# One of two transposed copies in a block inverse goes from TensorE to VectorE, and a list scheduler hands urgency on to whoever opens a tile

## The chip, the cores and the metric

The kernel runs on one core of a Trainium2 chip. The metric is device time in microseconds (us) per execution; a time shown for a kernel is the median of several runs. A core has five engines with queues of their own, each of which issues in order: TensorE (PE in the profile, its weight loads PEld), VectorE (DVE), ScalarE (ACT), GpSimd (POOL) and SyncE (SP, which issues the DMA transfers).

## The reference, cut to what matters

One decoder layer for 2048 prompt tokens and 8 single-token samples, width 1024: a mixer (a Conformer convolution beside a gated DeltaNet with 4 heads of 128), cross-attention into 256 memory tokens, a SwiGLU of inner width 2816, and a final norm. The change lies in the chunked DeltaNet, in chunks of 64 tokens:

```python
decay = jnp.exp(jnp.where(incl, gc[..., :, None] - gc[..., None, :], -jnp.inf))
lower = jnp.where(strict, jnp.einsum('nbhid,nbhjd->nbhij', kb, k) * decay, 0.0)
a_mat = lower + jnp.eye(c, dtype=lower.dtype)
u = lax.linalg.triangular_solve(a_mat, v * beta[..., None], left_side=True, lower=True, unit_diagonal=True)
w = lax.linalg.triangular_solve(a_mat, kb * jnp.exp(gc)[..., None], left_side=True, lower=True, unit_diagonal=True)

def step(s, xs):                      # over the chunks, state s
    v_new = u_i - jnp.einsum('bhcd,bhde->bhce', w_i, s)
    o_i = (jnp.einsum('bhcd,bhde->bhce', q_i * jnp.exp(g_i)[..., None], s)
           + jnp.einsum('bhij,bhje->bhie', qk_i, v_new))
    s = s * jnp.exp(g_last)[..., None, None] + jnp.einsum('bhcd,bhce->bhde', k_dec, v_new)
    return s, o_i
```

## The kernel before, in words

**Stages.** The prompt is cut into four blocks of 512 tokens. The matrix work runs on TensorE in this order: the input projection of blocks 0 and 1 and then of 2 and 3 (tiles `hd`, `glua`, `glub`); keys and values of the memory (`mkv`, `wk`, `vp`, with the transposes `pkt`); output projection and attention of blocks 0 and 1 (`rg`, `sc`, `ppt`); SwiGLU of block 0 (`fx`, `fy`, `fz`, then `dn`, `dx`, `dz`); attention of block 2; and so on to the SwiGLU of block 3. Weights come from DRAM into tiles `raw`, which ScalarE and VectorE or GpSimd split into two rounded parts `w`; each product is three matmuls.

**The DeltaNet in between.** For each of 4 heads and 4 blocks a generator `dn_front` (L1819) prepares four pieces of 128 tokens (NT = 4), and `dn_chain` (L2020) then carries the state through them one after the other. So there are 16 fronts and 64 steps of the chain. Their instructions are threaded between the matmuls of the stages above. A step of the chain is a row of links across engines: `pch<-S,kT` on TensorE, `chr` on VectorE, `pch<-chr,W` on TensorE, `chv` on ScalarE, `pch<-chv,..` on TensorE, the new state `S` on VectorE.

**The inverse.** A front solves the triangular system by inverting `a_mat` in tiles `Tm` (the inverse) and `W` (its transpose), both 128x512: first blocks of 16 on VectorE and GpSimd (`base_inverse`), then 32, 64 and 128 wide by two small matmuls per level (`pu1` and `pu2`, both `pu` in the profile). Before the levels from 32 and from 64 the transpose has to be made anew from `Tm`. A helper `renew` (L1939) does it: four 128x128 transposes on TensorE against the identity into a PSUM tile `ptw`, and one ScalarE copy of the 128x512 tile into `W`. It is called at L1969 and L1996. After the first call, `Tm` consists of blocks of 32 by 32 on the diagonal and zeros elsewhere. ScalarE copies behind each call put the pieces side by side.

**What sets the order.** Nothing is issued while the generators run: every instruction is recorded by the class `Tape`. `Tape.order` (L316) is a list scheduler with a planner's clock per engine; it picks, among the instructions that its clock has ready on an engine, the one with the smallest key, and `issue` (L524) then issues all of them in that order, so L530 is the line of nearly all instructions. The key of a TensorE instruction is its place in the recorded program. The key of any other is the smallest of its own place plus LATER = 300, the keys of its successors, and the keys of the instructions that wait for a buffer that it helps to free (`nxt`, in `keys`, L299). An instruction whose tile has no buffer yet opens one: pools are named by a tag and have a number of buffers (`t2` 28, `act` 22, `w` 6, `raw` 11 and small ones), and `may` (L351) lets a tile be opened ahead of earlier ones of its pool only if enough buffers stay for those. An addition, subtraction or product of two SBUF tiles may be given to GpSimd in place of VectorE if VectorE's backlog is over 1800 on the planner's clock.

Of the kernel before, what the change touches and what calls it, by code (L numbers as in the profile page):

```python
# [154 lines left out]
class Tape:  # L155
# [19 lines left out]
        return TapePort(self, real, eng)  # L175

    def add(self, eng, op, fn, args, kw):
        if op in ("matmul", "transpose", "memset"):
            outs, ins = [args[0]], [a for a in args[1:] if hasattr(a, "name")]
        else:  # L180
            outs = [kw[k] for k in ("out", "accum_out") if kw.get(k) is not None]
            ins = [v for k, v in kw.items() if k not in ("out", "accum_out") and hasattr(v, "name") and hasattr(v, "shape")]
        self.ops.append((eng, op, fn, args, kw, outs, ins, self.cost(eng, op, args, kw, outs, ins)))
        two = {"dve": "pool", "pool": "dve"}.get(eng)
        if two in self.real and op == "tensor_tensor" and kw.get("op") in (ALU.add, ALU.subtract, ALU.mult):
            if elems(outs[0]) >= FLEX and not any(a.name in self.psum for a in outs + ins):
                self.other[len(self.ops) - 1] = two, getattr(self.real[two], op), self.cost(two, op, args, kw, outs, ins)
# [108 lines left out]
            tiles.append(list(dict.fromkeys(a.name for a in outs + ins if a.name in self.tag_of)))  # L296
        return preds, tiles

    def keys(self, succs, line, first, tiles):  # L299


        N = len(self.ops)
        nxt = {}
        for tag, ts in line.items():
            for k, t in enumerate(ts[: -self.bufs[tag]]):
                nxt[t] = first[ts[k + self.bufs[tag]]]
        key = list(range(N))
        for n in range(N - 1, -1, -1):
            if self.ops[n][0] != "pe":
                after = [key[m] for m in succs[n]] + [key[nxt[t]] for t in tiles[n] if t in nxt and nxt[t] > n]  # L310
                key[n] = min([n + LATER, *after])
        for n in self.follow:
            key[n] -= N
        return key

    def order(self):  # L316
        from heapq import heapify, heappop, heappush

        preds, tiles = self.graph()
        N = len(self.ops)  # L320
        succs, left = [[] for _ in range(N)], [len(p) for p in preds]
# [13 lines left out]
        for tag, ts in line.items():  # L335
# [3 lines left out]
            for t in ts:  # L339
# [1 line left out]
                    heappop(held)  # L341
                heappush(held, last[t])
                live[tag].append(len(held))
        key = self.keys(succs, line, first, tiles)
        free = {tag: [0.0] * self.bufs[tag] for tag in line}
        head = dict.fromkeys(line, 0)
        early = {tag: set() for tag in line}
# [305 lines left out]
def hybrid_step(ctx: ExitStack, tc: tile.TileContext, i: dict, o: list):  # L653
# [1165 lines left out]
    def dn_front(h, b, sc, prev, out):  # L1819
# [146 lines left out]
            copy(lp[up, :, dn], lt[up, 0:NT:2, dn])  # L1966
            copy(lp[dn, :, up], lt[up, 1:NT:2, dn])
        yield Tm
        yield from renew()  # L1969
        for r in (0, 64):  # L1970
            up, dn = slice(r, r + 32), slice(r + 32, r + 64)
            copy(Tm[dn, 0:NT:2, up], Tm[up, 1:NT:2, up])
# [1224 lines left out]
```

## Time and profile before

| what | value |
|---|---|
| time, median of 3 runs | 2899.41 us (2897.57 to 2899.71) |
| the profiled execution: its time | 2901.18 us |
| the profiled execution: its span | 2899.4 us |
| PE busy | 2854.1 us, 98% of the span |
| DVE busy | 2438.3 us, 84% |
| ACT busy | 1534.5 us, 53% |
| POOL busy | 803.6 us, 28% |
| mean DMA rate | 196 GB/s |
| mean granted clock of TensorE | 0.996 |

The span runs from the first to the last instruction; the execution's own time has 1.8 us around it, and stands 1.8 us above the median of the runs. A busy share is the share of time in which at least one instruction of the engine is under way. Matmuls overlap one another, so a line of the groups with x4 and 0.60 us means four matmuls from the start of the first to the end of the last.

### The profile page before, as it was taken

What the parts mean: (1) busy time and instruction counts of PE and PEld (TensorE: products, weight loads), DVE (VectorE), ACT (ScalarE), POOL (GpSimd) and SP (SyncE); (2) the same over time, 40 slices, a digit from 0 to 9 for tenths busy, and PEclk for the clock granted to TensorE, in tenths of its full rate; (3) what the DMA queues carried; (4) which work ended last, traced back from release to release, by engine and by line L of the source; (5) the groups of instructions that cost most, each with busy time, mean ns of one, the idle gap of its engine ahead of it and who ended that gap; (6) DMA issues with size and microseconds to landing.
All of it is one profiled execution on the core that took longest, in us unless ns stands there. A gap on an engine that the chain in (4) does not pass through costs nothing. (4 is left out here: it accounts for less than half of the span.)

```text
span 2899.4 us, 55713 instructions
## 1 busy us (share of the span) xinstructions
PE 2854.1 (98%) x19302; PEld 2577.1 (89%) x19302; DVE 2438.3 (84%) x5311; ACT 1534.5 (53%) x3444; POOL 803.6 (28%) x965
## 2 busy tenths in 40 slices
PE   9999999999999999999999999999999999999998
PEld 8999878888788888898988789999889999999998
DVE  8859889898758959998888878888867888888888
ACT  7654564557675456475655454444554444444444
POOL 3311253216302026655213810000632242400000
PEclk9999999999999999999999999999999999999999
DMA  6433335777764426756777777777627666676673
GB/s 224 143 107 108 116 122 178 233 251 250 226 225 124 124 90 200 236 168 224 245 245 252 247 240 238 246 234 240 195 84 234 208 211 189 211 235 196 218 212 127
DMA packets 363035, 569.39 MB, mean 196 GB/s; under 512 B 55841, under 2 KB 158561, under 8 KB 362737
## 3 DMA queue, kind: packets, MB, share of 16 engines
q1 hardware_dynamic: 362752, 565.84, 61.0%
q8 instruction: 152, 2.49, 0.4%
q14 instruction: 131, 1.07, 0.1%
HBM read 457.77 MB, written 108.51 MB: 195 GB/s over the span
## 5 line engine op out<-in xcount | busy, mean ns | idle before, releaser
L530 ACT ACTIVATE w<-raw 128x512 fp32r<-128x512 f32 (+1 forms) x1066 | 649.0, 619 | 793.3 <-issue 133.7
L530 DVE TENSOR_TENSOR w<-raw,w 128x512 fp32r<-128x512 f32 (+1 forms) x842 | 593.2, 709 | 181.5 <-ACT w L530 172.2
L530 PE MATMUL fy<-op,w 128*128 128x256 f32 (+1 forms) x3168 | 435.6, 282 | 2.0 <-DMA w<-sums 2.0
L530 PEld LDWEIGHTS fy<-op,w 128*128 128x128 f32 x3168 | 399.9, 188 | 6.9 <-PE fz L530 2.0
L530 POOL TENSOR_TENSOR w<-raw,w 128x512 fp32r<-128x512 f32 (+1 forms) x224 | 311.8, 1397 | 317.5 <-ACT w L530 245.8
L530 PE MATMUL hd<-hT,w 128*128 128x512 f32 (+2 forms) x1920 | 386.3, 354 | 0.6 <-DVE hT L530 0.6
L530 DVE SCALAR_TENSOR_TENSOR cacc<-cu,cw,cacc 128x512 f32<-128x512 f32 x480 | 358.0, 746 | 5.5 <-ACT cacc L530 2.2
L530 PEld LDWEIGHTS hd<-hT,w 128*128 128x128 f32 x1920 | 304.5, 188 | 47.3 <-DVE hT L530 1.2
L530 PE MATMUL fx<-op,w 128*128 128x256 f32 (+1 forms) x2112 | 296.7, 283 | 1.0 <-ACT ffu L530 0.9
L530 PE MATMUL fz<-op,w 128*128 128x256 f32 (+1 forms) x2112 | 287.4, 283 | 1.3 <-DMA w<-sums 1.2
L530 PEld LDWEIGHTS fx<-op,w 128*128 128x128 f32 x2112 | 269.2, 189 | 6.5 <-issue 1.7
L530 PEld LDWEIGHTS fz<-op,w 128*128 128x128 f32 x2112 | 264.7, 188 | 6.2 <-DMA w<-sums 2.3
L530 PE MATMUL dx<-fo,w 128*128 128x256 f32 (+1 forms) x1344 | 198.3, 283 | 2.2 <-DVE x L530 2.2
L530 PE MATMUL dn<-ff,w 128*128 128x512 f32 (+2 forms) x960 | 193.4, 354 | 1.0 <-DVE x L530 0.9
L530 PE MATMUL rg<-pT,w 128*128 128x512 f32 x768 | 191.1, 400 | 1.1 <-ACT pr L530 0.8
L530 PE MATMUL sc<-w,hT 128*128 128x512 f32 x768 | 188.3, 399 | 3.1 <-ACT pr L530 2.7
L530 PE MATMUL rg<-catS,w 128*128 128x512 f32 (+2 forms) x960 | 187.6, 352 | 0.4 <-DVE x L530 0.4
L530 PEld LDWEIGHTS dx<-fo,w 128*128 128x128 f32 x1344 | 174.7, 188 | 5.0 <-DVE x L530 3.6
L530 PEld LDWEIGHTS rg<-catS,w 128*128 128x128 f32 x960 | 154.2, 188 | 24.7 <-DVE x L530 0.6
L530 PEld LDWEIGHTS sc<-w,hT 128*128 128x128 f32 x768 | 141.3, 188 | 36.5 <-ACT pr L530 5.1
L530 PEld LDWEIGHTS dn<-ff,w 128*128 128x128 f32 x960 | 151.6, 189 | 23.0 <-DVE x L530 2.1
L530 PEld LDWEIGHTS rg<-pT,w 128*128 128x128 f32 x768 | 140.6, 188 | 33.3 <-ACT pr L530 2.2
(433 smaller groups left out, 4901.4 us busy)
## 6 DMA issues: line engine op xcount, KB each, us to landing
w<-sums SPq DMA_DIRECT2D x222, 512.0 KB, 4.4
raw<-in_w_gate_dram SPq DMA_DIRECT2D x192, 256.0 KB, 3.7
sums<-w SPq DMA_DIRECT2D x66, 512.0 KB, 3.7
raw<-in_w_up_dram SPq DMA_DIRECT2D x118, 256.0 KB, 3.7
raw<-in_w_down_dram SPq DMA_DIRECT2D x224, 128.0 KB, 2.8
raw<-in_w_in_dram SPq DMA_DIRECT2D x96, 256.0 KB, 3.0
raw<-sums SPq DMA_DIRECT2D x74, 256.0 KB, 3.4
raw<-wk SPq DMA_DIRECT2D x64, 256.0 KB, 3.0
```

What stands on the lines that cost most here:

```text
L530: fn(*args, **kw)
```

## The change

Two edits go in together.

First, the call of `renew` at L1969 is replaced by one VectorE instruction that transposes each block of 32 by 32 of `Tm` where it lies, straight into `W`. The second call, at L1996, stays. So that the tape records a VectorE `transpose` by its keywords, `add` now asks whether positional arguments were given.

Second, `keys` gets the list `live` (how many tiles of the pool are open, in program order, when a tile is opened). For tile number k of a pool with `bufs` buffers it looks up the tile m = k + 1 + bufs - live[k], which is the first later tile that finds no room while tile k has not been opened, and puts the key of the instruction that opens tile m among those from which the opener of tile k takes the smallest. Openers on TensorE keep their place as key.

```diff
     def add(self, eng, op, fn, args, kw):
-        if op in ("matmul", "transpose", "memset"):
+        if args:
             outs, ins = [args[0]], [a for a in args[1:] if hasattr(a, "name")]
...
-    def keys(self, succs, line, first, tiles):
+    def keys(self, succs, line, first, tiles, live):
...
-        nxt = {}
+        nxt, bars = {}, {}
         for tag, ts in line.items():
             for k, t in enumerate(ts[: -self.bufs[tag]]):
                 nxt[t] = first[ts[k + self.bufs[tag]]]
+            for k, t in enumerate(ts):
+                m = k + 1 + self.bufs[tag] - live[tag][k]
+                if m < len(ts) and first[ts[m]] > first[t]:
+                    bars.setdefault(first[t], []).append(first[ts[m]])
         key = list(range(N))
         for n in range(N - 1, -1, -1):
             if self.ops[n][0] != "pe":
                 after = [key[m] for m in succs[n]] + [key[nxt[t]] for t in tiles[n] if t in nxt and nxt[t] > n]
+                after += [key[m] for m in bars.get(n, ())]
                 key[n] = min([n + LATER, *after])
...
-        key = self.keys(succs, line, first, tiles)
+        key = self.keys(succs, line, first, tiles, live)
...
         yield Tm
-        yield from renew()
+        V.transpose(out=W.rearrange("p c i -> p (c i)"), in_=Tm.rearrange("p c i -> p (c i)"))
         for r in (0, 64):
             up, dn = slice(r, r + 32), slice(r + 32, r + 64)
             copy(Tm[dn, 0:NT:2, up], Tm[up, 1:NT:2, up])
```

**What moves.** TensorE loses 64 of its 128 transposes `ptw`, ScalarE 16 of 32 copies `W<-ptw`, and VectorE gains 16 block transposes of 128x512. No other matmul and no transfer is added or dropped. The order differs on every engine in the first part of the program; it is the same again, instruction by instruction, over the last 9220 of 18386 matmuls, the last 2382 of 5313 VectorE instructions, the last 1042 of 3127 on ScalarE, the last 170 of 970 on GpSimd and the last 731 of 2062 transfers (counts of the order before).

**Place A, the first inverse that lies in the SwiGLU of block 0 (the twelfth of 16 before, the thirteenth now).** ScalarE before, with the copy that the change removes (`Tm` and `W` are the inverse and its transpose, `ffu`, `ffs` and `w` belong to the SwiGLU):

```order
L530 ACTIVATE lt_2672<-lt_2672 64x2x64
L530 ACTIVATE w_2853<-raw_2793 128x512
L530 ACTIVATE Tm_2771<-Tm_2771 32x2x32 x2
L530 ACTIVATE W_2816<-ptw_2852 128x512
L530 ACTIVATE W_2816<-W_2816 32x2x32 x2
L530 ACT_TABLE_LOAD
```

VectorE of the change, with the block transpose in its place:

```order
L535 TENSOR_TENSOR ffu_2961<-fz_2963,ffu_2961 128x256
L535 TENSOR_TENSOR Tm_2838<-pu_2766_2964,Tm_2838 128x16x16
L535 TENSOR_TENSOR w_2965<-raw_2920,w_2965 128x512
L535 STREAM_TRANSPOSE W_2936<-Tm_2838 128x512
L535 TENSOR_TENSOR ffs_2962<-ffu_2961,fy_2970 128x256
L535 TENSOR_REDUCE w_2741_2939<-Tm_2938 32x2x2 x2
```

The transpose now follows two instructions behind the sum that completes `Tm`, with one weight split between them, and stands ahead of the SwiGLU's eviction `ffs<-ffu,fy`.

**Place B, a step of the chain behind that inverse, in the same SwiGLU.** TensorE before, at the third of the chain's four steps (`pch` and `po` are the chain, `pkk`, `pqk`, `pu` and `ptw` the fronts, `fy` and `dn` the SwiGLU):

```order
L530 MATMUL pch_2960<-S_2956,kT_2668 128x128
L530 MATMUL pkk_2965<-kT_2916 128x128 x4
L530 MATMUL pch_2960<-chr_2961,W_2816 128x128
L530 MATMUL fy_2933<-op_2529,w_2928 128x256
L530 MATMUL fy_2933<-op_2541,w_2928 128x256 x3
L530 MATMUL fy_2933<-op_2555,w_2928 128x256 x2
L530 MATMUL po_2897<-chv_2967,dn_2667 128x128
L530 MATMUL pu_2770_2968<-u_217,W_2935 128x64 x4
L530 MATMUL pch_2960<-chv_2967,dn_2666 128x128
L530 MATMUL pqk_2971<-qTd_2917,kT_2916 128x128 x4
L530 MATMUL ptw_2973<-ident,Tm_2834 128x128 x4
L530 MATMUL pch_2974<-S_2969,kT_2668 128x128
```

TensorE of the change, at the first step of the chain behind the inverse of place A:

```order
L535 MATMUL pch_3024<-S_1437,kT_2696 128x128
L535 MATMUL dn_3020<-ff_2990,w_2999 128x512 x3
L535 MATMUL dn_3027<-ff_2942,w_2999 128x512 x3
L535 MATMUL dn_3027<-ff_2990,w_2999 128x512 x3
L535 MATMUL pu_2830_3028<-Tm_2938,lo_3026 64x64 x4
L535 MATMUL dn_3030<-ff_2942,w_3000 128x512 x3
L535 MATMUL pch_3024<-chr_3025,W_2936 128x128
L535 MATMUL dn_3030<-ff_2990,w_3000 128x512 x3
L535 MATMUL dn_3032<-ff_2942,w_3000 128x512 x3
L535 MATMUL dn_3032<-ff_2990,w_3000 128x512 x3
L535 MATMUL pu_2835_3033<-u_217,W_2976 128x64 x4
L535 MATMUL fx_3035<-op_2593,w_3002 128x256 x3
```

Between the first two links of the step there stood four short matmuls; now there stand twelve long ones and four short ones.

**Place C, the values of the memory (`vp`).** TensorE before, at a step of the chain beside the ninth inverse:

```order
L530 MATMUL pch_1929<-S_1914,kT_1520 128x128
L530 MATMUL po_1887<-S_1914,rb_1525 128x128
L530 MATMUL ptw_1931<-ident,Tm_1740 128x128
L530 MATMUL vp_1879<-w_1871,kvT_1752 128x512 x3
L530 MATMUL vp_1879<-w_1873,kvT_1752 128x512 x3
L530 MATMUL vp_1881<-w_1871,kvT_1752 128x512 x3
L530 MATMUL vp_1881<-w_1873,kvT_1752 128x512 x3
L530 MATMUL vp_1896<-w_1892,kvT_1752 128x512 x3
L530 MATMUL vp_1896<-w_1895,kvT_1752 128x512 x3
L530 MATMUL ptw_1931<-ident,Tm_1740 128x128 x3
L530 MATMUL pch_1929<-chr_1930,W_1736 128x128
L530 MATMUL lnp_1960<-ident,lnx_1928 128x128 x4
```

TensorE of the change, again at a step beside the ninth inverse:

```order
L535 MATMUL po_1886<-chv_1904,at_1485 128x128
L535 MATMUL pch_1940<-S_1916,kT_1477 128x128
L535 MATMUL pu_1734_1932<-u_217,W_1765 128x64 x2
L535 MATMUL po_1886<-S_1916,rb_1482 128x128
L535 MATMUL pch_1940<-chr_1941,W_1655 128x128
L535 MATMUL ptw_1944<-ident,Tm_1673 128x128 x4
L535 MATMUL po_1886<-chv_1948,at_1485 128x128
L535 MATMUL pch_1940<-chv_1948,kd_1483 128x128
L535 MATMUL pu_1757_1955<-Tm_1673,lt_1585 128x64 x2
L535 MATMUL po_1886<-S_1953,rb_1482 128x128
L535 MATMUL vp_1901<-w_1879,kvT_1736 128x512 x3
```

Here 18 long matmuls stood between two links; now a whole step of the chain passes with no long matmul in it.

**Counted over the whole order.** Each of the 64 steps has two round trips from TensorE back to TensorE (from `pch<-S` over `chr` to `pch<-chr`, and from there over `chv` to `pch<-chv`), 128 in all. With 0.23 us for a matmul of 512 columns, 0.12 for one of 256 and 0.11 for the short ones (the distances between their starts in the trace), 14 round trips have less than 1.1 us of TensorE work between their links before, and 7 with the change. Of the 14, six lie in the SwiGLU of block 0; of the 7, none does. In the stretch of `mkv`, `wk` and `vp` there are 3 before and 4 with the change.

## The prediction, as it was recorded before the result

> **What bounds the kernel now.** I read the engines' shares first, then the busy time by stretches, then the waits of TensorE, and last the lines of the inverse in order of time.
>
> ```profile
> PE 2854.1 (98%) x19302; PEld 2577.1 (89%) x19302; DVE 2438.3 (84%) x5311; ACT 1534.5 (53%) x3444; POOL 803.6 (28%) x965
> ```
>
> TensorE sits idle for 2899.4 - 2854.1 = 45.3 us in all. Nothing that shortens another engine can give more than that; only work taken from TensorE itself, or a lost clock given back, goes beyond it. The stretches say where the idle time lies (columns: PE, PEld, DVE, ACT, POOL busy with counts, granted clock, DMA share, GB/s):
>
> ```profile
> 0.00:1500.00 1500.00, 1473.37 (x9047) 1280.08 (x9048) 1276.89 (x2635) 893.55 (x2130) 501.92 (x722) 0.99 0.57 182
> 1500.00:1600.00 100.00, 99.88 (x599) 85.30 (x599) 85.45 (x138) 53.23 (x119) 32.59 (x28) 1.00 0.76 256
> 1600.00:2800.00 1200.00, 1191.13 (x8910) 1122.68 (x8909) 988.92 (x2317) 544.09 (x1104) 265.26 (x211) 1.00 0.67 213
> 2800.00:2900.00 100.00, 89.69 (x752) 89.04 (x750) 87.07 (x225) 43.59 (x93) 3.86 (x5) 0.97 0.49 153
> ```
>
> Of the idle time, 26.6 us lie before 1500 us, where the DeltaNet runs, 8.9 between 1600 and 2800, and some 10 in the last 100. The order of the change equals the old one over the last 9220 matmuls; 8910 + 752 are issued after 1600 us, so from about 1700 us on nothing is moved. TensorE is busy for 1191.1 of 1200 us there: what is won or lost earlier should come through to the end whole, as a shift.
>
> Within the first part the idle time is uneven, and the granted clock falls short of one in four stretches:
>
> ```profile
> 300.00:400.00 100.00, 96.79 (x565) 79.17 (x565) 85.69 (x179) 59.67 (x148) 44.27 (x66) 0.98 0.40 122
> 600.00:700.00 100.00, 99.63 (x522) 82.70 (x521) 91.45 (x177) 64.12 (x140) 29.03 (x35) 0.98 0.80 255
> 700.00:800.00 100.00, 92.48 (x557) 79.73 (x556) 75.73 (x156) 67.50 (x164) 52.23 (x70) 0.97 0.78 246
> 800.00:900.00 100.00, 97.67 (x687) 89.28 (x687) 71.49 (x155) 66.97 (x159) 15.44 (x23) 1.00 0.60 196
> 1100.00:1200.00 100.00, 97.65 (x616) 87.11 (x614) 97.70 (x165) 55.96 (x131) 70.60 (x65) 1.00 0.72 235
> 1200.00:1300.00 100.00, 97.71 (x731) 91.30 (x730) 95.85 (x200) 63.72 (x167) 55.02 (x76) 1.00 0.63 195
> 1300.00:1400.00 100.00, 97.21 (x670) 88.28 (x669) 90.26 (x180) 56.69 (x145) 54.06 (x57) 0.98 0.63 214
> ```
>
> The worst stretch, 700 to 800 us, is the memory's keys and values (`wk`, `vp`): 7.5 us idle and 3% of the clock. In the SwiGLU of block 0, 1100 to 1300, VectorE is nearly full.
>
> **The transposes that leave TensorE.** The first `ptw` of the trace, in order of time:
>
> ```profile
> 147.45 0.60 PE L530 MATMUL ptw<-ident,Tm 128*128 128x128 f32 x4
> 147.88 0.60 PE L530 MATMUL pq<-ident,qTd 128*128 128x128 f32 x4
> ```
>
> One transpose lasts 0.27 us, but the next group starts 147.88 - 147.45 = 0.43 us after the first, so four of them hold TensorE for 0.43. Sixteen such groups go: 16 x 0.43 = 6.9 us. TensorE is 98% busy in the first 1500 us, so this comes off the path almost whole: **-6.9**. ScalarE loses 16 copies:
>
> ```profile
> L530 ACT ACTIVATE W<-ptw 128x512 f32<-128x512 f32 x32 | 19.2, 599 | 0.7
> ```
>
> That is 16 x 0.60 = 9.6 us on an engine that is 53% busy. It is worth nothing by itself; what it does for the round trips is in the term after next.
>
> **The block transposes that come to VectorE.** No such instruction is in the trace. The nearest rows, 128x256 below and 128x512 above (last but one number: mean ns):
>
> ```profile
> L530 DVE TENSOR_TENSOR raw<-hd,rsb 128x256 f32<-128x256 f32 x24 | 9.4, 414 | 3.7 <-PE hd L530 3.7
> L530 DVE TENSOR_REDUCE scs<-kt 128x2 f32<-128x512 f32 x32 | 20.9, 673 | 4.8 <-POOL kt L530 4.8
> L530 DVE SCALAR_TENSOR_TENSOR xn<-xn,vcol,rsb 128x512 f32<-128x512 f32 x2 | 2.7, 1371 | 0.0
> ```
>
> I take 0.67, the row with one SBUF source and 512 elements; the ends are 0.41 and 1.37. So 16 x 0.67 = 10.8 us (6.6 to 21.9) against 1500 - 1276.9 = 223 us of idle VectorE: covered, but not where VectorE is 96 to 98% busy. Four of the inverses lie in that SwiGLU in the new order. There the transpose stands ahead of `ffs<-ffu,fy` (place A), which frees a PSUM tile that TensorE's next `fx`, `fy` or `fz` needs. If each delays TensorE by its whole length, that is 4 x 0.67 = 2.7 us (5.5 by the upper row); if none does, 0. The transpose's own wait, for the sum that completes `Tm`, is two places ahead on the same engine with a weight split between them, so nothing queues behind an open wait. Even with VectorE full, TensorE was idle for only 2.3 us per 100 there, which speaks for the lower end: **+1.0**.
>
> By the Trainium skill, "VectorE: DVE Perf Modes", section "The three transpose paths", a 128x128 block transpose of 16-bit numbers takes 311 ns on VectorE; four for a 128x512 tile would be an estimate of 1.24 us. No run here shows one. By that the term would be 4 x 1.24 = 5.0 at most and 1.9 in the same proportion, and the sum 0.9 less favourable.
>
> **The round trips.** What TensorE waited for in the DeltaNet (us in total, times, longest):
>
> ```profile
> PE pu L530 <- DMA Tm<-zt: 2.2, 2, 1.5
> PE po L530 <- ACT chv L530: 1.6, 2, 1.1
> PE pch L530 <- DVE chr L530: 1.6, 3, 1.2
> PE pch L530 <- DVE S L530: 1.3, 1, 1.3
> PE ptw L530 <- ACT Tm L530: 1.3, 4, 0.5
> PE pu L530 <- DVE u L530: 0.8, 2, 0.4
> ```
>
> Together 8.8 us. How long a round trip needs, seen where one just fails to fit:
>
> ```profile
> 796.85 0.38 PE L530 MATMUL pch<-S,kT 128*128 128x128 f32 x2
> ...
> 798.03 0.49 PE L530 MATMUL pch<-chr,W 128*128 128x128 f32 x2 [0.19 <-DVE chr L530]
> 798.96 0.43 PE L530 MATMUL pu<-u,W 128*128 128x64 f32 x2 [0.43 <-DVE u L530]
> 799.51 0.49 PE L530 MATMUL po<-chv,at 128*128 128x128 f32 x2
> ```
>
> From start to start 1.18 us over VectorE, so about 1.1 us of other matmuls must stand between two links. In the old order 14 of 128 trips have less, and the missing pieces add up to 6.9 us (3.1 over `chr`, 3.8 over `chv`); in the new order 7 have less, with 3.3 us missing (2.7 and 0.6). The trips of place B are gone; place C has a new one, with 0.3 and 0.5 us where there were 4.7 and 0.5. The ends: 0, if something else fills the gap, and -8.8, if all of these waits go. I take the difference, 3.3 - 6.9: **-3.6**. What would be late next is the weight split that TensorE's next product needs, since the chain no longer holds it back.
>
> **The clock.** Two places where it was lost:
>
> ```profile
> 747.00:753.00 6.00, 3.25 (x24) 2.81 (x25) 5.96 (x16) 2.34 (x6) 3.49 (x5) 0.99 0.34 100
> 753.00:757.00 4.00, 4.00 (x23) 4.00 (x22) 4.00 (x9) 1.47 (x4) 2.60 (x2) 0.58 0.61 215
> 1310.00:1316.00 6.00, 4.47 (x21) 3.37 (x21) 6.00 (x11) 2.54 (x6) 6.00 (x5) 1.00 0.24 71
> 1316.00:1320.00 4.00, 4.00 (x15) 3.41 (x16) 4.00 (x7) 0.00 (x0) 0.77 (x3) 0.57 0.90 294
> ```
>
> After 6 us in which TensorE was busy for only 3.3 or 4.5, the next 4 us are granted 0.57 to 0.58: 1.7 us lost each time. The four stretches above lose 2 + 2 + 3 + 2 = 9 us in all. Which of them come back under the new order the order doesn't tell; I take **0**, with ends of -9 and +5 (three more).
>
> By the Trainium skill, "TensorE: Matmul & The Clock Gate", section "Why this matters for your kernels", the clock falls only for idle gaps over some 3 us. The trace disagrees here, since it fell after pieces of at most 1.3 us:
>
> ```profile
> 748.08 0.49 PE L530 MATMUL pch<-S,kT 128*128 128x128 f32 x2 [1.34 <-DVE S L530]
> 751.20 0.66 PE L530 MATMUL pkt<-ident,kv 128*128 128x128 f32 x4 [1.23 <-ACT kv L530]
> ```
>
> By that rule no rearrangement could win or lose clock, and the rivals below would lose their clock terms.
>
> **The sum.** -6.9 + 1.0 - 3.6 + 0 = -9.5 us. The profiled execution took 2901.18 us, 1.8 around its span of 2899.4; it would take 2891.7. The median of the runs is 1.8 below the profiled one: 2889.9, or 0.33% less. A difference under 0.2%, 5.8 us, can't be told from none here.
>
> **The rivals.**
>
> *More is won.* All 8.8 us of those waits go, and with them three of the clock losses: -6.9 - 8.8 - 3 x 1.7 = -20.8, 2878.6 us. For it: the SwiGLU loses all its tight trips, and four inverses lie there where there were five, under a VectorE that was full. Against it: seven tight trips stay, four of them in the worst stretch.
>
> *Nothing is won.* The loosened trips don't count, because the link behind them is late on VectorE anyway (0); the transposes cost their full 2.7 in the full SwiGLU; one clock loss comes on top (1.7): -6.9 + 2.7 + 1.7 = -2.5, 2896.9. That is also the case in which the new keys do nothing useful. For it: every reordered queue meets its waits anew, and the planner's clock knows nothing of the granted clock. Against it: 6.9 us leave the bounding engine for certain.
>
> *Slower.* The crowding at `wk` and `vp` decides. In the new order the ninth inverse and a whole step of the chain stand there with no long matmul among them (place C), and two tight trips lie in `wk`. From 700 to 900 us, 7.5 + 2.3 us were idle and 3 us of clock lost; if that stretch loses the same again, it is 12.9 us more: -6.9 + 1.0 + 12.9 = +7.0, 2906.4. It decides as soon as the stretch loses over 5.9 us more, about half of what it loses now. For it: the clock falls exactly behind such small idle pieces. Against it: the stretch holds as many steps of the chain as before, six, and one tight trip more.
>
> **How the numbers follow.** The forecast (-4 to -16) has 0.50, of which 0.04 lies within 0.2%; more won 0.14; nothing won 0.22; slower 0.14. So faster 0.46 + 0.14 = 0.60, same 0.04 + 0.22 = 0.26, slower 0.14. The range runs from 2877, which leaves out the better half of the larger gain (0.06), to 2903, which leaves out most of the slower case (0.10). The forecast's own range is 2883 to 2896.
>
> **What would show it.** `ptw` shows 64 matmuls in place of 128 and `W<-ptw` 16 copies; TensorE's busy time falls by some 7 us less what is idle now and filled then; a block transpose takes 0.4 to 1.4 us, most likely 0.67. Idle time before `pch`, `po`, `ptw` and `pu` falls from 8.8 to some 5 us, and none of it lies in the SwiGLU. From 1700 us on the two traces differ by a constant shift. It is wrong if the stretch of `wk` and `vp` shows over 13 us idle or a clock under 0.97, if the block transpose lasts over 1.4 us, or if the second half stretches by more than 3 us.

## The result, and the profile after

The change took **2921.6 us** (median of 6 runs, 2917.0 to 2924.6) against 2899.6 for the kernel before beside it (6 runs): a ratio of **1.0069, 95% interval 1.0059 to 1.0079**, some 20 us slower. The forecast was 2889.9, faster. The profiled span grew from 2899.4 to 2919.2 us, by 19.8.

The engines' shares, of the changed kernel:

```profile
PE 2854.9 (98%) x19238; PEld 2575.5 (88%) x19238; DVE 2482.6 (85%) x5316; ACT 1525.7 (52%) x3427; POOL 822.0 (28%) x976
```

64 matmuls are gone, and yet TensorE is busy for 0.8 us longer (2854.1 before): what was saved is used up by a lower clock. It is idle for 2919.2 - 2854.9 = 64.3 us, where it was 45.3. The stretches say where (PE, PEld, DVE, ACT, POOL busy with counts, granted clock, DMA share, GB/s). Before:

```profile
0.00:600.00 600.00, 593.64 (x3551) 509.06 (x3552) 511.21 (x1116) 348.03 (x792) 172.70 (x321) 1.00 0.49 155
600.00:950.00 350.00, 339.44 (x2011) 291.22 (x2010) 279.92 (x583) 229.03 (x540) 101.59 (x137) 0.99 0.68 217
950.00:1350.00 400.00, 390.91 (x2397) 342.48 (x2396) 352.49 (x671) 222.17 (x575) 178.49 (x207) 1.00 0.53 169
1350.00:1700.00 350.00, 346.30 (x2127) 299.89 (x2126) 306.12 (x541) 193.97 (x444) 147.96 (x130) 1.00 0.71 239
1700.00:2800.00 1100.00, 1094.07 (x8475) 1045.40 (x8474) 901.51 (x2180) 497.66 (x1002) 199.04 (x165) 1.00 0.67 213
```

And with the change:

```profile
0.00:600.00 600.00, 595.37 (x3590) 510.54 (x3591) 515.70 (x1121) 355.28 (x819) 180.94 (x323) 1.00 0.49 156
600.00:950.00 350.00, 328.31 (x1942) 282.72 (x1941) 289.14 (x578) 215.77 (x536) 163.12 (x202) 0.98 0.68 213
950.00:1350.00 400.00, 382.69 (x2242) 330.97 (x2241) 358.03 (x643) 204.34 (x500) 132.17 (x147) 0.99 0.51 163
1350.00:1700.00 350.00, 344.80 (x2163) 301.13 (x2163) 308.83 (x547) 200.86 (x466) 140.32 (x132) 1.00 0.71 237
1700.00:2800.00 1100.00, 1095.21 (x8408) 1042.99 (x8407) 907.32 (x2164) 497.40 (x997) 201.58 (x168) 1.00 0.67 213
```

From 600 to 950 us (the end of the second input projection; the memory's `mkv`, `wk` and `vp`, up to 823 us; then output projection and attention) TensorE is busy for 11 us less. From 950 to 1350 (output projection and attention, and from 1144 us before or 1169 now the first half of the SwiGLU of block 0) it is 8 less. Below, the first of the two is called the memory's stretch. Behind 1700 us little changed. A second thing moved: GpSimd has 202 instructions in the memory's stretch, where it had 137, and 147 in the next, where it had 207. Work of the DeltaNet's fronts has come forward. The matmuls `pkk<-kT`, of which each front issues 8, count the fronts. Before:

```profile
600.00:950.00 350.00, 3.22 (x24) 2.91 (x24) 3.34 (x12) 0.99 0.68 217
950.00:1350.00 400.00, 4.39 (x32) 3.98 (x32) 4.54 (x16) 1.00 0.53 169
```

With the change:

```profile
600.00:950.00 350.00, 5.38 (x40) 4.93 (x40) 5.70 (x20) 0.98 0.68 213
950.00:1350.00 400.00, 2.11 (x16) 1.94 (x16) 2.33 (x8) 0.99 0.51 163
```

Five fronts are prepared in the memory's stretch in place of three, two in the next in place of four. What TensorE waits for now (us in total, times, longest):

```profile
PE pu L535 <- DMA Tm<-zt: 6.3, 3, 4.7
PE fz L535 <- DMA w<-sums: 4.1, 5, 1.5
PE fx L535 <- ACT ffu L535: 3.5, 3, 1.9
PE pqk L535 <- DVE vnk L535: 3.4, 1, 3.4
PE mkv L535 <- ACT kv L535: 3.3, 1, 3.3
...
PE pk L535 <- DVE lt L535: 2.6, 1, 2.6
...
PE dnb L535 <- DVE tbd L535: 2.2, 1, 2.2
...
PE pch L535 <- DVE S L535: 1.0, 1, 1.0
PE pch L535 <- DVE chr L535: 0.7, 2, 0.4
...
PE ptw L535 <- ACT Tm L535: 0.5, 1, 0.5
```

The chain's waits did shrink: `pch`, `po` and `ptw` from 5.8 us to 2.2. In their place stand a few long single waits in the fronts and around them. (Of the 4.1 us of `fz`, 3.1 lie behind 1700 us.) How one comes about, in order of time, on VectorE:

```profile
713.12 0.74 DVE L535 SCALAR_TENSOR_TENSOR cacc<-cu,cw,cacc 128x512 f32<-128x512 f32 x1
713.77 4.84 DVE L535 CAST catS<-hcat 128x8 fp32r<-128x8 f32 x1
718.39 0.82 DVE L535 SCALAR_TENSOR_TENSOR cacc<-cu,cw,cacc 128x512 f32<-128x512 f32 x1
...
720.79 0.68 DVE L535 TENSOR_TENSOR vnk<-pvv,s 128x512 f32<-128x512 f32 x1
```

on GpSimd:

```profile
713.39 1.29 POOL L535 TENSOR_TENSOR w<-raw,w 128x512 fp32r<-128x512 f32 x1
714.63 0.12 POOL L535 MEMSET w<- 32x16 f32 x1
714.70 1.26 POOL L535 TENSOR_TENSOR w<-raw,w 128x512 fp32r<-128x512 f32 x1
715.93 1.27 POOL L535 TENSOR_TENSOR catS<-cat,catS 128x512 fp32r<-128x512 f32 x1
717.17 1.27 POOL L535 TENSOR_TENSOR w<-raw,w 128x512 fp32r<-128x512 f32 x1
```

and on TensorE:

```profile
717.59 0.55 PE L535 MATMUL pu<-u,W 128*128 128x64 f32 x4
721.52 0.83 PE L535 MATMUL pqk<-qTd,kT 128*128 128x128 f32 x3 [3.38 <-DVE vnk L535]
```

A cast of 8 columns lasts 4.84 us on VectorE, up to 718.61. GpSimd's run of four subtractions of 128x512 ends at 717.17 + 1.27 = 718.44, and the cast 0.17 us behind it, which is as long as such a cast takes alone (first series below). The front's `vnk` stands four instructions behind it, and TensorE stands still for 3.4 us. The clock follows:

```profile
717.00:722.00 5.00, 1.62 (x11) 1.35 (x10) 5.00 (x8) 1.49 (x5) 3.05 (x5) 0.97 0.63 216
722.00:726.00 4.00, 4.00 (x20) 3.83 (x20) 3.64 (x11) 1.32 (x4) 0.00 (x0) 0.60 0.60 151
```

Below, an instruction of VectorE is called **held** if it lasts over 2.4 us before 1700 us; the changed kernel has 6 (23.8 us together), the one before 1 (3.7 us). The **loss** of a stretch is TensorE's idle time in it and half of the time for which the clock records show half speed, which comes in steps of 3.4 us. Up to 1700 us the loss went from 38.2 to 64.2 us, 26.0 more; 5.8 us of TensorE's work (busy time less half of the half-speed time) go off, and 0.4 us less is lost behind 1700. That makes the 19.8 by which the span grew. By stages, in us, with the fronts that start in each:

| stage, and where it ends (before / now) | loss before | loss now | fronts before / now |
|---|---|---|---|
| up to 600 | 8.1 | 4.6 | 7 / 7 |
| input projection, to 689 / 684 | 2.1 | 2.0 | 0 / 1 |
| `mkv`, to 748 / 749 | 1.3 | 10.1 | 2 / 1 |
| `wk` and `vp`, to 823 | 11.2 | 7.8 | 0 / 0 |
| output projection and attention, to 950 | 1.1 | 10.4 | 1 / 3 |
| the same, to 1144 / 1169 | 1.7 | 7.4 | 1 / 0 |
| SwiGLU of block 0, to 1350 | 9.1 | 15.0 | 3 / 2 |
| up to 1700 | 3.7 | 6.9 | 2 / 2 |

The loss grows on both sides of `wk` and `vp`, and not in them.

### The profile page after: what moved, and what is told of

It is laid out like the page before. It is cut to its first block, busy times and chain, and to the rows that moved or that the text cites. A ratio compares the mean times of both kernels' runs of the same rounds, so it can differ in the third digit from the quotient of the medians.

```text
span 2919.2 us, 55627 instructions
## 1 busy us (share of the span) xinstructions
PE 2854.9 (98%) x19238; PEld 2575.5 (88%) x19238; DVE 2482.6 (85%) x5316; ACT 1525.7 (52%) x3427; POOL 822.0 (28%) x976
## 5 line engine op out<-in xcount | busy, mean ns | idle before, releaser
L535 DVE TENSOR_TENSOR w<-raw,w 128x512 fp32r<-128x512 f32 (+1 forms) x847 | 606.9, 720 | 152.5 <-ACT w L535 147.7
L535 PEld LDWEIGHTS fz<-op,w 128*128 128x128 f32 x2112 | 265.0, 188 | 10.8 <-DMA w<-sums 5.6
```

Of the source, the lines that this page charges most:

```text
L535: fn(*args, **kw)
```

## The experiments

In the expectations theory P has VectorE held behind GpSimd's runs, theory K has the new keys cost time whatever they act on, and theory S has any rearrangement move the time by chance. Each kernel is compared with the kernel before on its own chip; times in brackets are 95% intervals of the ratio.

**Each part alone, and the lateness bound.** The transposes alone leave the new rule out:

```diff
-                after += [key[m] for m in bars.get(n, ())]
```

> The block transpose alone, with the old keys. Measured so far: 2899.6 us before, 2921.6 with both edits; TensorE idle 45.3 us before, 64.3 after; five half-clock stretches of 3.4 us before 1700 us, then nine. Theory K (the handed-on urgency orders the work badly): 2893 us, the 6.9 us of transposes less some 1 us. Theory T (the transposes on VectorE hold up its queue): 2915 us or more. Theory P (a VectorE instruction is held for 3 to 5 us while GpSimd runs instructions back to back; TensorE waits behind it and its clock halves; how often the two meet is set anew by any other order): the time follows the number of VectorE instructions held over 3 us before 1700 us, of which the kernel before has 1 and the change 6.

The keys alone put the old call back:

```diff
-        V.transpose(out=W.rearrange("p c i -> p (c i)"), in_=Tm.rearrange("p c i -> p (c i)"))
+        yield from renew()
```

> The handed-on urgency alone, with the transposes left on TensorE. Theory K: 2928 us, 6.9 more than with both edits. Theory T: 2899 us or less. Theory P: between 2895 and 2930, and again by the number of held instructions.

Two kernels have neither part, only `LATER = 310` or `290`:

> The kernel before, with LATER = 310 in place of 300: the same work, another order, neither edit. Theory N (any other order loses, since the one before is an unusually good one): 2910 us or more. Theories K and T: 2899 +- 6 us. Theory P: the time follows the number of held VectorE instructions, whichever way it goes.

> The kernel before, with LATER = 290: a second order without either edit. Theory N: 2910 us or more, as with 310. Theories K and T: 2899 +- 6 us. Theory P: by the number of held VectorE instructions.

Then the changed kernel, and the transposes alone, at the other bounds:

> Both edits with LATER = 290. The kernel before took 2916.9, 2901.9 and 2894.9 us with LATER = 290, 300 and 310. Theory K (the handed-on urgency costs time by itself): above the old keys for each value of LATER, here 2925 us or more. Theory R (every order is a draw, with some 10 us of spread, and the new keys are one more): anywhere from 2895 to 2925, not tied to the 2916.9.

> Both edits with LATER = 310. Theory K: 2908 us or more, over the 2894.9 of the old keys with 310. Theory R: anywhere from 2895 to 2925; at or below 2895 would speak against K outright.

> The block transpose alone with LATER = 310, against the 2894.9 us of LATER = 310 without it. If the 6.9 us of TensorE come through: 2888 us. Theory R: 2885 to 2915, since the edit also re-orders everything around it, as with LATER = 300, where it gave nothing (2901.4 against 2901.9).

> Old keys, VectorE's transpose, lateness bound 290: the third pair beside the new keys with the transpose at 290 (2914.6 us). Theory K (the new keys cost 10 to 20 us whatever the order they act on: plus 20 at 300, plus 11 at 310): 2895 to 2905. Theory S (an order's time is spread by chance over some 25 us and the bound of 290 is simply a bad one for the old keys, 2916.9 without the transpose): 2908 to 2918, no more than 7 us from both.

And the keys alone at 310:

> The new keys with TensorE's transposes kept and the lateness bound at 310; the old keys at 310 took 2894.9 us. A second pair without the transposes. Theory K (the new keys cost 10 to 20 us whatever they act on): 2904 to 2916, with 3 held VectorE instructions or more and TensorE's idle time before 1700 us at 34 us or above. Theory S (chance of the order): as near to 2895 as to 2915, 2890 to 2903 being as likely as not.

Measured, ratio to the kernel before and median in us:

| LATER | neither | transposes alone | keys alone | both |
|---|---|---|---|---|
| 290 | 1.0055 (1.0040 to 1.0070), 2916.9 | 1.0013 (1.0004 to 1.0023), 2903.5 | not run | 1.0044 (1.0028 to 1.0060), 2914.6 |
| 300 | 1 | 1.0005 (0.9992 to 1.0017), 2901.4 | 1.0058 (1.0043 to 1.0073), 2918.0 | 1.0069, 2921.6 |
| 310 | 0.9975 (0.9966 to 0.9985), 2894.9 | 1.0006 (0.9997 to 1.0016), 2902.1 | 1.0022 (1.0013 to 1.0032), 2907.2 | 1.0038 (1.0023 to 1.0053), 2912.9 |

A bound moved by 10 in 300, with nothing else changed, moves the time by -7 or +16 us: two rearrangements that aim at nothing move it that far. The new keys cost in all five pairs, by the ratios 9, 19 and 9 us with the transposes and 17 and 14 without. So theory K stands as a direction for these five pairs, with a size that the order sets; the neutral orders scatter as widely, so that the keys must cost time in any order is not shown. Most sizes that were expected missed: theory K's 2893 and 2928 for the parts alone, its 2925 or more for both at 290, its three held instructions for the keys alone at 310 (there was one), and the 2888 for the transposes at 310. Theory T failed both ways, and theory N, which fits 290, failed at 310. The transposes with the order made anew are worth -12, +1 and +9 us on the old keys, +3 and +5 on the new ones: no gain on average, where 6.9 us leave TensorE by the prediction's sum. Losses by stretch in the profiled executions (us), with the fronts in the memory's stretch:

| kernel | fronts, 600 to 950 | GpSimd instructions there | loss 600 to 950 | loss 950 to 1350 | held |
|---|---|---|---|---|---|
| neither, 290 / 300 / 310 | 3 / 3 / 3 | 145 / 137 / 136 | 13.6 / 15.7 / 12.6 | 22.5 / 10.8 / 9.2 | 2 / 1 / 1 |
| keys alone, 300 / 310 | 3 / 3 | 142 / 141 | 14.4 / 17.2 | 26.4 / 16.3 | 3 / 1 |
| transposes alone, 290 / 300 / 310 | 5 / 5 / 5 | 190 / 191 / 188 | 20.4 / 27.2 / 20.0 | 13.5 / 15.8 / 16.3 | 2 / 2 / 1 |
| both, 290 / 300 / 310 | 5 / 5 / 5 | 204 / 202 / 201 | 28.3 / 30.2 / 29.2 | 16.9 / 22.4 / 20.7 | 8 / 6 / 2 |

(For the transposes alone at 290 and 300 the profiled execution lay 8 us above the median, so their losses stand too high; at 310 it did not.) This table holds the two causes apart. The transposes, whatever the bound and the keys, bring two more fronts into the memory's stretch, and it loses 7 to 16 us more. The keys cost another 8, 3 and 9 us there, on top of the five fronts; with three fronts they cost nothing clear there (-1 and +5), but 16 and 7 us from 950 to 1350.

**The exchange in place.** Here the order of the kernel before is kept, instruction by instruction; as they are issued, the 64 transposes and 16 copies are dropped and the block transpose is put where the first of a tile's four stood:

```diff
...
+                if n in self.swap:
+                    W, Tm = self.swap[n]
+                    if W.name not in self.swapped:
+                        self.swapped.add(W.name)
+                        flat = "p c i -> p (c i)"
+                        self.real["dve"].transpose(out=W.rearrange(flat), in_=Tm.rearrange(flat))
+                    continue
...
```

> The kernel before, every instruction in the order that it had, with one thing exchanged as the instructions are issued: the 64 TensorE transposes and the 16 ScalarE copies are left out, and one VectorE block transpose per tile stands where the first transpose of that tile stood. It parts the exchange itself from the new order that the scheduler makes around it. Theory A (the exchange is worth what the sum said, 6.9 us of TensorE time and a little for the round trips; what ate it in the kernel with the transposes alone, at 2901.4 beside 2901.9, was the order): 2890 to 2895 us beside 2899.5, ratio 0.9970 to 0.9985, TensorE idle before 1700 us within 3 us of 28.5. Theory B (the time is lost again wherever the exchange is made, since TensorE at these places waits for the rest of the chain): 2898 to 2901, idle before 1700 us up by 5 us or more, to 34 or above.

> The same exchange in place, on the order that the old keys give with the lateness bound at 310 in place of 300 (2894.9 us by itself, 4 to 7 us under the kernel before). Theory A: the two add, 2885 to 2890 us, ratio to the kernel before 0.9945 to 0.9965. Theory B: 2893 to 2897, ratio 0.9975 to 0.999.

Measured: 0.9992 (0.9984 to 1.0001), 2898.0 us; and on the order of 310, 0.9967 (0.9957 to 0.9977), 2891.7, where that order alone gave 0.9975. Both are 2.3 us under their own base by the ratios, the first with an interval from 0 to 5: between the theories, and by the idle time nearer to B. The memory's stretch in the first and, for comparison, in the transposes alone:

```profile
600.00:950.00 350.00, 338.84 (x2002) 290.32 (x2001) 284.81 (x590) 227.20 (x540) 101.85 (x139) 0.99 0.69 218
```

```profile
600.00:950.00 350.00, 333.03 (x1960) 287.31 (x1959) 275.81 (x584) 217.12 (x539) 154.57 (x191) 0.97 0.67 212
```

With the order kept there is no damage. But TensorE's busy time falls only from 2854.1 to 2849.0 us, by 4.8 at equal clock (4.4 in the other pair), and before 1700 us its idle time, counted from its first matmul at 1.2 us, rises from 28.5 to 32.1 (24.7 to 28.3 in the other): TensorE comes sooner to work whose data are no sooner there, and a part of what it no longer does becomes waiting. The second kernel is the best of the study, 0.33% faster than the kernel before.

**Runs of GpSimd broken.** Of the changed kernel, 15 instructions of 128x512 that GpSimd ran at four of the places with held instructions are issued on VectorE, at the same place of the order:

```diff
...
+                if n in self.other and self.given[n] == "pool" and outs[0].name in BREAK:
+                    self.given[n] = "dve"
```

> The change, with 15 of GpSimd's 128x512 instructions given back to VectorE at the four places (685 to 696, 711 to 719, 862 to 870, 898 to 908 us) where a VectorE instruction of the change is held for 3.4 to 4.8 us while GpSimd runs back to back; everything else keeps its place. Theory P (the held instructions make the stalls of TensorE just behind them: 3.4, 3.5, 4.8 and 2.2 us, and three of the clock losses, 6.8 us): the holds are gone from the trace and the time falls by 12 to 20 us, to 2902 to 2910 us, though VectorE does 15 x 0.7 = 10.5 us more. Rival (the holds lie beside the path, the DeltaNet's pieces come late for another reason): 2917 to 2926 us, and stalls of TensorE over 3 us at the same places.

The control gives back fifteen others of the same kinds and stretch, where nothing is held:

> The changed kernel with fifteen other GpSimd instructions of 128x512 given back to VectorE at the same place of the order: out of the same stretch (640 to 900 us) and of the same kinds, also from runs, but where no VectorE instruction is held. Theory P (the fifteen at the held places gave 15.7 us because they broke the holds): 2915 to 2923 us, five or more holds left. Theory G (GpSimd takes 1.3 us where VectorE takes 0.7, and the gain is that pace, wherever it is had): 2903 to 2910.

And the same on the other order of the new keys, for the 22 beside its eight held instructions:

> Both parts with the lateness bound at 290 (2914.6 us, eight VectorE instructions held for 32.6 us), and the 22 GpSimd instructions of 128x512 that ran while one of them was held given back to VectorE, in the same place of the order. Theory P: 12 to 20 us less, 2895 to 2903, two holds or fewer. Theory G': the gain of the first such kernel was its own order's luck: 2909 to 2917 with the holds gone.

Measured: 2905.9 (1.0024, 1.0012 to 1.0035), 13 us less than the changed kernel by the ratios and 15.7 by the medians, with 1 held instruction left; the control 2922.2 (1.0076, 1.0061 to 1.0091), no gain, 6 held; the second order 2897.8 (0.9995, 0.9986 to 1.0005), 14 us less by the ratios and 16.8 by the medians, 2 held of 8. The memory's stretch of the first:

```profile
600.00:950.00 350.00, 335.89 (x2009) 288.24 (x2008) 292.81 (x628) 227.30 (x566) 150.79 (x190) 0.99 0.70 220
```

of the control:

```profile
600.00:950.00 350.00, 326.44 (x1925) 281.58 (x1925) 291.42 (x593) 215.87 (x537) 145.22 (x185) 0.97 0.66 212
```

VectorE is busy for 291 to 293 us in both, and GpSimd is relieved in both (163.1 us with the change as it is); in the memory's stretch TensorE gains 7.6 us in the one and loses 1.9 in the other. So it is the place of the runs that counts, not GpSimd's pace. TensorE's waits agree. With the runs broken:

```profile
PE pu L538 <- DMA Tm<-zt: 3.7, 3, 2.8
```

in the control:

```profile
PE pu L538 <- DMA Tm<-zt: 6.2, 2, 5.3
...
PE pqk L538 <- DVE vnk L538: 3.4, 1, 3.4
...
PE mkv L538 <- ACT kv L538: 3.3, 1, 3.3
```

Of the changed kernel's four waits behind held instructions at these places, `mkv` 3.3, `pqk` 3.4, `pu` 4.7 and `dnb` 2.2 us, the first kernel has `pu` alone left, with 2.8; the control has all four (3.3, 3.4, 5.3 and 2.2). Theory P is shown for these two orders, and what breaking the runs gives is most of what the keys add there, though it was not tried on the old keys: with the runs broken, the new keys with the transposes stand 5.5 us above the transposes alone at 300 and 5 below at 290. It is not the whole of K: at 310 the keys cost 9 and 14 us with 2 and 1 held instructions, at most one more than without them. Nor does the count of held instructions order the kernels by itself: two stand beside a cost of 16 us (neither part, 290) and two beside 1 us (the transposes alone, 300).

**Which openings.** The rule moves 82 openings of the pool of 28 work tiles directly, 21 of the weights `w`, 4 of other pools. One kernel each lets only one pool hand on urgency:

```diff
-                if m < len(ts) and first[ts[m]] > first[t]:
+                if m < len(ts) and first[ts[m]] > first[t] and tag[1] == "t2":
```

> VectorE's transpose, and urgency handed on only by those who open a tile of the pool of 28 work tiles (82 openings that the rule moves, against 21 of the weight pool and 4 of two others). Theory K1 (the work tiles' openings cost the time: evacuations and loads of the DeltaNet and the convolution come ahead of the weights' products): 2912 to 2924. Theory K2 (the weight pool's openings cost it: weight products are put ahead of the work tiles, and GpSimd gets them in runs): 2898 to 2906 here.

> VectorE's transpose, and urgency handed on only by the openings of the weight pool (21 that the rule moves). The work tiles' openings alone gave 2907.9 us, the transpose alone 2901.4, all openings 2921.6. Theory K3 (the two pools' openings add up to the 20 us): 2911 to 2917. Theory K4 (each rearrangement moves the time by some 5 to 10 us of chance, and the two do not add): 2897 to 2908.

Measured: 2907.9 (1.0032, 1.0020 to 1.0044) for the work tiles, 4 held; 2901.6 (0.9998, 0.9989 to 1.0008) for the weights, 3 held. Against the transposes alone (1.0005) that is +8 and -2, and all together +19: they do not add. The first result lies between both of its theories; the second favours K4. Which opening costs the rest stays open.

**What holds VectorE.** Two kernels append short series behind the last instruction, in which both engines start from the same ScalarE copy:

> The kernel before with eight short stretches appended behind its last instruction, some 100 us in all, where GpSimd runs 0, 1, 2, 4 or 8 instructions of 128x512 back to back and VectorE, released by the same ScalarE copy, runs a series of its own: a 128x512 product from SBUF, a 128x8 cast, a 128x8 product, a 128x512 scaling, four times over. Three more with eight: VectorE with casts and scalings alone (one source each); VectorE with products of a PSUM source; GpSimd with copies (one source) in place of products. Theory P (VectorE's instruction is held until GpSimd's run of two-source instructions ends): the longest VectorE instruction grows with the run, about 1.4, 2.8, 5.6 and 11 us for 1, 2, 4 and 8, casts of 128x8 included, and none over 1 us beside GpSimd's copies. Theory R (held for a bounded time, two or three of GpSimd's instructions, however long the run): 3 to 5 us for both 4 and 8. Theory Q (no hold: each VectorE instruction is only slowed by what the other takes): none over 1.5 us at any length, and the holds of 3.4 to 4.8 us in the changed kernel need another cause.

GpSimd's eight products beside VectorE's mix, and VectorE's groups in that stretch:

```profile
2924.32 11.13 POOL L3138 TENSOR_TENSOR pqa<-pqb 128x512 f32<-128x512 f32 x8
```

```profile
L3146 DVE TENSOR_TENSOR dqa<-dqb 128x512 f32<-128x512 f32 x4 | 4.9, 1228 | 0.1
L3147 DVE CAST dqr<-dqh 128x8 fp32r<-128x8 f32 x4 | 4.0, 1001 | 0.0
```

Alone the product took 0.69 us and the cast 0.17. Beside GpSimd the cast takes 1.00 and the product 0.68 to 1.41, and nothing takes longer, for a run of 1, 2, 4 or 8: the engines take turns, and VectorE never waits for more than one of GpSimd's instructions. This is theory Q; by P as it was put, the cast would have waited for up to 11 us. In the program it is otherwise: the six held instructions of the changed kernel all end within 0.6 us of the end of a run of GpSimd, after two or three of its instructions that began later than they did. All six stand right behind the convolution's accumulation in PSUM (`cacc`, as the cast above), and so do 38 of the 47 held instructions in the traces of the 18 kernels without appended series, where 480 of some 2900 VectorE instructions before 1700 us are such accumulations. The second series tried that:

> The kernel before with twelve short stretches appended, in each of which GpSimd runs eight products of 128x512 back to back (in the first six on one tile, in the rest on tiles of their own, each written over one of its sources, in the type of the weights), while VectorE runs six times: an accumulation of a scaled SBUF tile in PSUM and a cast; two accumulations and a cast; an accumulation and a product; the same operation from SBUF to SBUF and a cast; a product of a PSUM source and a cast; an accumulation, a fill of growing length and a cast. In the program 18 of 21 held instructions stand right behind the convolution's accumulation in PSUM, where some one in six would by chance. Theory C (that predecessor is the cause): 2.4 to 5 us for the cast or product behind an accumulation, in the first three series at least, and none over 1.5 us behind the operation from SBUF to SBUF. Theory C' (GpSimd's tiles are: no wait between its instructions on tiles of their own): none over 1.5 us in the first six, 2.4 us and more in the last six, whatever stands before. Theory R (chance of arrival): none over 1.5 us anywhere.

VectorE's groups over the whole of it, 48 accumulations `pqs<-dqb,dqh,pqs` among them:

```profile
L3155 DVE CAST dqr<-dqh 128x8 fp32r<-128x8 f32 x54 | 40.2, 744 | 0.0
L3152 DVE SCALAR_TENSOR_TENSOR pqs<-dqb,dqh,pqs 128x512 f32<-128x512 f32 x48 | 35.8, 746 | 0.2
L3158 DVE TENSOR_TENSOR dqa<-dqb 128x512 f32<-128x512 f32 x24 | 22.8, 949 | 0.2
```

No instruction lasted over 1.83 us, behind whatever. Theories C and C' fall. Theory R, chance of arrival, is what is left, though six instructions passed its 1.5 us. That VectorE is held in the program, until GpSimd's run ends, and that TensorE pays for it, is shown; what makes it lose its turn there is not.

## Why the prediction was wrong

**The failing step is what the sum said of the new order: -3.6 us for the round trips of the chain, and nothing else.** It left the rest of TensorE's idle time and the clock as they were, and had no other term for the new keys. At a bound of 300 the runs show +1 us for the transposes with the order made anew and +19 for the keys on top of them (+17 without them), where the whole sum had -9.5; 13 of these 19 went when 15 of GpSimd's instructions beside held ones of VectorE were moved. The term rested on a count of chain steps and tight trips. The fronts were not counted, though the order shows them: five between 600 and 950 us for three. "The stretch holds as many steps of the chain as before, six" was held against the slower rival; what had changed were the fronts around it, one more ahead of `mkv`, one fewer beside it and two more behind `vp`. TensorE's idle time before 1700 us, from its first matmul on, rose from 28.5 to 47.6 us.

**The transposes, -6.9.** Mis-sized: the 0.43 us were read from the first group, and most groups of four take 0.35 to 0.36 from their start to that of the next matmul, as the second one does before (166.45 - 166.09):

```profile
166.09 0.60 PE L530 MATMUL ptw<-ident,Tm 128*128 128x128 f32 x4
166.45 1.33 PE L530 MATMUL hd<-hT,w 128*128 128x256 f32 x9
```

So 16 x 0.36 = 5.8 us leave, which is what the change shows at equal clock; in place it is 4.4 to 4.8, and TensorE gives 3.6 of them back as idle time. The run gains 2.3 (0 to 5). "Comes off the path almost whole" took a busy share of 98% for a guarantee.

**The block transposes, +1.0.**

```profile
L535 DVE STREAM_TRANSPOSE W<-Tm 128x512 f32<-128x512 f32 x16 | 11.3, 704 | 0.2
```

0.70 us each against 0.67 taken; the estimate of 1.24 from the Trainium skill ("VectorE: DVE Perf Modes", "The three transpose paths") is not borne out for this type and shape. What the sum lacked is that the exchange also takes out of the recorded program the places where a front waits for a PSUM tile and for the copy. With the order kept, three fronts stay in the memory's stretch; with it made anew, five come. That the missing waits are the reason is argued, not shown.

**The round trips, -3.6.** Right in sign for the waits it spoke of: `pch`, `po` and `ptw` 5.8 to 2.2 us. "What would be late next is the weight split" was wrong in the main: late next were the fronts, `pu` for its transfer with 6.3 us (2.2 before), `pqk` and `pk` for VectorE; waits for a weight split by ScalarE grew by 2.5 us. One wait of 4.7 us for `Tm<-zt`, at 876.9 us, is more than the whole term; on VectorE a step of an inverse (`w<-Tm`) had stood right behind a held weight split (864.9 to 869.0 us).

**The clock, 0.** The half-speed time before 1700 us grew from 17.1 to 30.7 us, so 6.8 us more were lost, past the upper end of +5. To avoid such drops the Trainium skill ("TensorE: Matmul & The Clock Gate", "Why this matters for your kernels") says to leave no idle gaps over some 3 us. Three of the seven drops now come with gaps of 3.3, 3.4 and 4.7 us, in line with it, but four follow pieces of at most 2.6 us.

**The slower rival** had the sign, and its test came true: 700 to 900 us shows 14.8 us idle (over the 13 named) at a clock of 0.95 and 0.97, and the loss there grew by 10.0 us (13.3 to 23.3), over the 5.9 named and near its price of 12.9. That is in part luck of the window. `wk` and `vp`, where it saw the crowding, lose less than before, 7.8 us for 11.2; what grew lies in `mkv` ahead of them and in the output projection and attention behind them. Its mechanism, a step of the chain with no long matmul, was not the one, and it lacked the stretch from 950 to 1350, with another 11.6. The larger gain's argument, that the SwiGLU would be relieved, failed as well: the SwiGLU of block 0 has four fronts for five and no tight trip, and yet TensorE is idle in it for 15.5 us (1169 to 1574 us), where it was 8.1 (1144 to 1555).

**Right:** the counts (64 `ptw`, 16 copies), the transposes' length, and the shift behind 1700 us: 18.6 us there, 19.7 at the end and never under 16.3 between them.

## What to carry to other kernels

When a scheduler orders the whole program, a small edit is two edits: what it does in place, and the new order. Measure the first with the order held, and before believing a gain of a few us, see how far a neutral nudge of the scheduler moves the time; two nudges here gave -7 and +16 us. In reading a new order, count every kind of work that a stretch receives, and look for runs on GpSimd ahead of short VectorE instructions that TensorE needs soon.

## What the runs showed of the hardware

VectorE and GpSimd, both on SBUF, take turns in the first series: a cast of 0.17 us takes 1.00 beside GpSimd, whose own eight products take 11.1 us in place of 8.9. The 8.9 were measured beside VectorE products with a PSUM source, which took 0.69 us each and met no delay. The Trainium skill, "SBUF — State Buffer", "Who interferes with whom", describes one holder for the whole instruction, and no contention for a VectorE instruction with at most one SBUF input outside the fast modes. The products with a PSUM source agree with it. That an instruction is passed over two or three times, for 3.4 to 4.8 us in the changed kernel, the program's traces show; the two series did not bring it about.
